# A two-layer transformer trunk: the Fourier stage's squares summed by TensorE, its additions by VectorE, none of them on GpSimd

## The chip, the cores and the metric

The kernel runs on one core of a Trainium2 chip. The metric is the device time of one execution in microseconds (us), given as the median of several runs. Five engines work at once, each through its own queue in order: TensorE (PE in the profile, its weight loads PEld), VectorE (DVE), ScalarE (ACT), GpSimd (POOL) and SyncE (SP), which issues most transfers.

## The reference

Two layers over 512 tokens of 1024 channels. Layer 0 is attention and a gated feed-forward network with a width-3 convolution; layer 1 is a Fourier mixer and another such network. Every sub-layer stands between two RMS norms. What this case touches is the end of layer 0 and the start of layer 1:

```
def rms_norm(x, g):
    y = xf * lax.rsqrt(jnp.mean(xf * xf, axis=-1, keepdims=True) + EPS)
    return (y * g.astype(F32)).astype(x.dtype)
...
def fourier_mix(h):
    hg = h.reshape(b, l, FNET_GROUPS, d // FNET_GROUPS).astype(F32)
    f = jnp.fft.fft2(hg, axes=(1, 3), norm="ortho").real
...
    x = x + g2 * rms_norm(conv_ffn(h, ...), norm_g[0, 3])        # end of layer 0
    h = modulate(rms_norm(x, norm_g[1, 0]), sh1, sc1)            # start of layer 1
    y = fourier_mix(h) @ w_f
```

All values are 32-bit floats.

## The kernel before

Activations lie transposed: 128 partitions hold 128 channels, the 1024 channels are 8 chunks (k = 0..7), and the 512 tokens run along the free axis in two halves of 256. The stream is `xT`, a sub-layer's output `yT`. For precise products each operand is split into a rounded part and a remainder (`hh`, `hl`; `wh`, `wl`; `zh`, `zl`), and `mm3` (L104 to L106) issues three matmuls into one PSUM tile. The PSUM pool has six tiles named `mm` and two named `misc`. A scheduler puts the written program into one order for each engine; `fence`, `held` and `follow` pin a few instructions.

**End of layer 0.** `ffn` ends with the down projection of its last group: eight output chunks `part(d)`, 8 x 3 matmuls of 128x256 each. All first halves (and d = 0 whole) come first. Then `mid(ys)` is called, and only after it in the written program stand the second halves of d = 1..7, 7 x 24 = 168 matmuls:

```
            if end:
                mid(ys)
                for d in range(1, KC):
                    part(d, [1])
```

Here `mid` is `plain.tiles(y, 0, 0, 3, pps, n1[0])`, the first token half's passage into layer 1. `ys.sums` has TensorE add up the squares of y (L187), `stat_bcast` turns them into a factor for each token (L205 to L209, L230, spread over partitions by the matmul L233, copied by ScalarE at L234), and for each chunk k:

- `x_update`: L317 scales y into `md_t` on VectorE, L319 adds it to `xT`, on VectorE for even k and on GpSimd for odd k in this first half;
- L372 (ScalarE) and L373 (VectorE) write the scaled new x, split into `hh` and `hl`;
- L380 (ScalarE) squares the new x, and L382 (GpSimd) adds the squares of chunks 1 to 6 into `yT[:, 0]`; chunks 0 and 7 are kept in `yT[:, 0]` and `yT[:, 7]`.

`columns` later sums these two tiles over the channels with four matmuls against a column of ones (L392), and `rstd` makes of them one factor for each token, with tokens on the partitions: the norm's factor is multiplied in only after the first Fourier product.

**Fourier stage.** `over_channels(g, h)` is the product over channels of group g and token half h (24 matmuls for the two token chunks of a half); `shift` computes the modulation's constant share (12 small matmuls, their inputs named `sh`); `group` and `cosines` are the products over tokens, for the first half's tokens (`[0, 1]`) and then for the second's (`[2, 3]`). The second half's `plain.tiles(ys, 1, ..., V)` runs between the first half's products, pumped piece by piece; there all of L319 is on VectorE already. The second half's Fourier products need no norm factor, but its tables do (`tables(1, r1)`, L1530 and L1531), so `columns(1)` stands ahead of them.

Last, `fourier_weights(d)` for d = 0..7 adds and subtracts two 128x512 blocks of the output weights (L1591 and L1592; L1591 by GpSimd but for d = 0), splits the result (L127, 128x1024), and 27 matmuls make output chunk d; L1651 and L1655 write it, and `ys.add` squares it on ScalarE (L290) and adds it up on GpSimd (L292, d = 1..5). GpSimd also issues the transfers of the next layer's first weights there (L1148, L1152, L1158).

Of the kernel before, what the change touches and what calls it, by code (L numbers as in the profile page):

```python
# [10 lines left out]
F32 = mybir.dt.float32  # L11
# [3 lines left out]
AF = mybir.ActivationFunctionType  # L15
ALU = mybir.AluOpType
# [3 lines left out]
P = 128  # L20
D = 1024
KC = D // P
T = 512
TT = T // P
HT = T // 2
# [56 lines left out]
def kernel(ctx: ExitStack, tc: tile.TileContext, a):  # L82
    nc = tc.nc
    V, S, G, PE, SY = nc.vector, nc.scalar, nc.gpsimd, nc.tensor, nc.sync
# [3 lines left out]
    def mk(pool, shape, dt=F32, tag=None, bufs=1):  # L88
        cnt[0] += 1
        n = nbufs.setdefault((id(pool), tag), (pool, bufs))[1]  # L90
        return pool.tile(shape, dt, tag=tag, name=f"{tag}_{cnt[0]}", bufs=n)
# [17 lines left out]
    def follow(i, j):  # L109
        tc.add_manual_dep(i.ins, j.ins.name, mybir.DependencyInfo(  # L110
            mybir.DependencyClass.NoSync, mybir.DependencyReason.DATA), reason="order")
# [19 lines left out]
    cp = ctx.enter_context(tc.tile_pool(name="cp", bufs=1))  # L131
# [14 lines left out]
    xT = mk(cp, [P, KC, T], F32, "xT")  # L146
    yT = mk(cp, [P, KC, T], F32, "yT")
# [3 lines left out]
    ones32 = mk(cp, [P, 32], F32, "ones32")  # L151
# [50 lines left out]
    def rstd(ps):  # L202
        w = ps.shape[1]
        v, t, r = (mk(cp, [P, W4], F32, "st_" + c, n)[:, :w] for c, n in (("v", 2), ("t", 1), ("r", 2)))
        S.activation(out=r, in_=ps, func=AF.Abs_reciprocal_sqrt, bias=eps, scale=1.0 / D)  # L205
        V.tensor_scalar(out=v, in0=ps, scalar1=1.0 / D, scalar2=EPS, op0=ALU.mult, op1=ALU.add)
        V.tensor_tensor(out=t, in0=r, in1=r, op=ALU.mult)
        V.scalar_tensor_tensor(out=t, in0=t, scalar=-0.5, in1=v, op0=ALU.mult, op1=ALU.mult)
        V.scalar_tensor_tensor(out=v, in0=t, scalar=1.5, in1=r, op0=ALU.add, op1=ALU.mult)  # L209
        return v  # L210
# [136 lines left out]
    class Plain:  # L347

        def __init__(self):
            self.acc = yT[:, 0, :]  # L350
            self.last = yT[:, KC - 1, :]

        def tiles(self, ys, h, l, gi, pps, am, urgent=False, eng=None, pe=False):
            hs = halves[h]
            ps = ys.sums(pps, h)
            if urgent:
                warm = mk(pps, [P, T], F32, "mm", 6)
                for s, n in zip(halves, HOT2):
                    busy(warm, ys.sq[:, s], n)
            R = stat_bcast(ps, pps)  # L360
            if urgent:
                busy(warm, R, HOT2[2])
            if pe and h == 0:
                self.ps = mk(pps, [P, T], F32, "mm", 6)
            yield
            for k in range(KC):
                i = x_update(h, l, gi, R, k, eng)
                if urgent and k == 1:
                    follow(i[0], j)
                j = i[1]  # L370
                x = xT[:, k, hs]
                S.activation(out=hh[:, k, hs], in_=x, func=AF.Copy, scale=am[:, k:k + 1])  # L372
                V.scalar_tensor_tensor(out=hl[:, k, hs], in0=x, scalar=am[:, k:k + 1], in1=f(hh[:, k, hs]),  # L373
                                       op0=ALU.mult, op1=ALU.subtract)
                if pe:
                    stat_x(self.ps[:, h * W4:], h, k)
                else:
                    sq = mk(cp, [P, T], F32, "sq", 2)[:, :HT] if 0 < k < KC - 1 else (self.last if k else self.acc)[
                        :, hs]
                    S.activation(out=sq, in_=x, func=AF.Square)  # L380
                    if 0 < k < KC - 1:
                        G.tensor_tensor(out=self.acc[:, hs], in0=self.acc[:, hs], in1=sq, op=ALU.add)  # L382
                if k % 2:
                    yield


        def columns(self, h, pps):
            ps = mk(pps, [P, T], F32, "misc", 2)
            for i in range(2):
                t = 2 * h + i  # L390
                for n, s in enumerate((self.acc, self.last)):
                    PE.matmul(ps[:, 2 * i:2 * i + 2], lhsT=s[:, t * P:(t + 1) * P], rhs=ones32[:, :2], start=n == 0,  # L392
                              stop=n == 1)
            return rstd(ps[:, :4])

        def rows(self, h):
            return rstd(self.ps[:, h * W4:(h + 1) * W4])
# [165 lines left out]
    def pump(it, n=1):  # L563
        for _ in range(n):
            next(it, None)
# [12 lines left out]
    with ExitStack() as es:  # L578
# [27 lines left out]
        with ExitStack() as e1:  # L606
            pj = e1.enter_context(tc.tile_pool(name="pj", bufs=1, reuse_waits="tile"))
            pps = e1.enter_context(tc.tile_pool(name="pps", bufs=1, space=PSUM, reuse_waits="tile"))
# [47 lines left out]
            for n in range(WARM):  # L656
                PE.matmul(warm[:, :256], lhsT=maskb[:, 0, :], rhs=maskb.rearrange("p a b -> p (a b)"), start=True,
                          stop=True)
# [100 lines left out]
            for s in START.split():  # L759
                n = [int(c) for c in s[1:]]  # L760
# [71 lines left out]
            for ps, (sh, sl, t, b) in zip(acc, tiles):  # L832
# [3 lines left out]
                if sh is ch:  # L836
                    sq = mk(cp, [P, T], F32, "sq", 2)[:, :256]
                    S.activation(out=sq, in_=src[:, 0, :], func=AF.Square)
                    V.tensor_tensor(out=dst.rearrange("p t (h d) -> p (t h) d", d=P),
                                    in0=src.rearrange("p t (h d) -> p (t h) d", d=P),  # L840
                                    in1=gqk[:, P:2 * P].unsqueeze(1).to_broadcast([P, 2, P]), op=ALU.mult)
# [48 lines left out]
            for g, kind in enumerate(["kb", "vb", "qa"]):  # L890
# [5 lines left out]
                for sh, sl, t0, kb in (blocks if kind[0] != "q" else blocks[:2]):  # L896
                    ps = mk(pps, [P, 2, 256], F32, "mm", 6)
# [26 lines left out]
        with ExitStack() as e2:  # L924
# [80 lines left out]
            for head in range(8):  # L1005
# [6 lines left out]
                for j in range(TT):  # L1012
                    qs = slice(j * P, (j + 1) * P)
                    ps = S0.pop() if S0 else mk(aps, [P, 1024], F32, "S", 2)
                    pr = mk(at, [P, NK], F32, "P", 7)
                    mx = mk(at, [P, 6], F32, "mx", 6)
                    if is_a:
# [4 lines left out]
                        reg, n = ps[:, 128:896], NK  # L1022
                    else:
# [9 lines left out]
                        for n_, (mi, off) in enumerate(mt):  # L1033
                            PE.matmul(ps[:, 512 + off:512 + off + P], lhsT=identb, rhs=maskb[:, mi, :],
                                      start=False, stop=n_ == len(mt) - 1)
                        reg, n = ps[:, 256:512 + nl], TC + nl
# [30 lines left out]
                    i = 4 * (head - 6) + j  # L1067
# [22 lines left out]
    pps = ctx.enter_context(tc.tile_pool(name="fps", bufs=1, space=PSUM, reuse_waits="tile"))  # L1090
    n0 = (der[:, 0, 2, :], mods[:, 0, 3, :])
    n1 = (der[:, 1, 0, :], mods[:, 1, 0, :])
# [377 lines left out]
    with ExitStack() as es:  # L1470
        xp = Pairs(es).rest(es)
        ys = out_proj(xp, ys, ow)
        plain = Plain()
        ys = ffn(0, xp, [], lambda: pump(boundary(ys, 1, 0, 1, pps, n0), 100),
                 lambda y: pump(plain.tiles(y, 0, 0, 3, pps, n1[0]), 6),
                 gemv_jobs([(1, v) for v in range(5)], pps, away))


    with ExitStack() as es:
# [103 lines left out]
            SY.dma_start(out=r, in_=a["w_f"][d])  # L1583
            return r

        def fourier_weights(d, eng=G):
            r = f_first[d] if d < 2 else raw([P, 4, 2, P], a["w_f"][d])

            pm = (yT[:, 6:8, :] if d in (3, 5) else yT[:, 2:4, :] if d == 1 else mk(cp, [P, 2, T], F32, "gacc")).rearrange(
                "p a (g c) -> p a g c", g=4)  # L1590
            held(eng.tensor_tensor(out=pm[:, 0, :, :], in0=r[:, :, 0, :], in1=r[:, :, 1, :], op=ALU.add))  # L1591
            held(V.tensor_tensor(out=pm[:, 1, :, :], in0=r[:, :, 1, :], in1=r[:, :, 0, :], op=ALU.subtract))  # L1592
            wh, wl = wpair([P, 2, 4, P])
            split(wh, wl, pm)
            return wh, wl
# [28 lines left out]
        group(2, [2, 3])  # L1624
        fence()
        group(0, [2, 3])
        w_f = [fourier_weights(0, V)]
        group(1, [2, 3])
        cosines(None, N, [z[:, :, :, P] for z in Z], list(range(TT)), fb[:4, 4:5])
        group(3, [2, 3])  # L1630
# [33 lines left out]
    with ExitStack() as es:  # L1664
# [13 lines left out]
        for k in range(0, KC, 2):  # L1678
            t = mk(cp, [P, T], F32, "sq", 2).rearrange("p (a b) -> p a b", a=2)
# [97 lines left out]
```

## Time and profile before

| | |
|---|---|
| median of 3 runs | 1136.24 us (1133.64 to 1137.02) |
| the profiled execution's own time | 1138.32 us |
| its span in the trace | 1136.5 us |
| TensorE matmul busy | 1098.6 us, 97% |
| VectorE busy | 902.6 us, 79% |
| ScalarE busy | 592.9 us, 52% |
| GpSimd busy | 174.9 us, 15% |
| mean granted TensorE clock | 0.991 |

A row of the engines' timeline reads: start in us from the span's start, duration in us, engine, line, operation, output<-inputs, shapes, count, and in brackets how long the engine had been idle before it and what released it. A matmul's end is modelled, so back-to-back matmuls overlap in these rows; their spacing is what they cost. A 32-bit matmul that isn't split appears as two passes. A row of the windows view reads: stretch, length, and busy time with the count of instructions of PE, PEld, DVE, ACT and POOL, then the granted clock, the DMA share and GB/s. A row of the groups reads: line, engine, operation, names, shapes, count, busy us, mean ns of one, and idle us before them.

### The profile page before, as it was taken

The page shows a single profiled execution, that of the slowest core. Times are in us where ns is not written, and L with a number is a line of the kernel's source. Part 1 is how long each engine was busy: PE and PEld are TensorE (multiplying, and loading weights), DVE is VectorE, ACT ScalarE, POOL GpSimd, SP SyncE. Part 2 cuts the span into 40 slices and gives each one's busy share as a digit, 9 for nine tenths or more (in the row PEclk, how much of TensorE's full clock was granted, in tenths as well). Part 3 has the DMA queues.
Part 4 walks back from the last instruction along what each step waited for, and adds up shares of the span by engine and source line. Part 5 has one row for each costly group of instructions (what it writes and reads, how often), then busy time and mean ns, then how long its engine had stood idle before and what let it go on. Part 6 is the DMA issues. An engine that isn't in the chain of part 4 may idle for free.

```text
span 1136.5 us, 19542 instructions
## 1 busy us (share of the span) xinstructions
PE 1098.6 (97%) x7810; PEld 962.9 (85%) x7810; DVE 902.6 (79%) x1469; ACT 592.9 (52%) x1056; POOL 174.9 (15%) x180
## 2 busy tenths in 40 slices
PE   9999899999999999999999999889999999999995
PEld 5689888868898978887998998779888898899995
DVE  5678777773789976978998568878997998879755
ACT  4342355665665633552555446557745555555543
POOL 1136422422320000000000153610000000000012
PEclk9999999999999999999999999899999999999998
DMA  9676101174142455536425302732114523222332
GB/s 365 262 238 216 38 1 39 53 274 156 63 162 111 156 204 203 181 131 236 187 75 204 103 20 75 206 114 108 74 47 160 192 103 116 103 89 95 105 144 75
DMA packets 33764, 155.83 MB, mean 137 GB/s; under 512 B 3461, under 2 KB 8197, under 8 KB 22025
## 3 DMA queue, kind: packets, MB, share of 16 engines
q1 hardware_dynamic: 32520, 150.39, 36.8%
q0 software_dynamic: 1152, 4.19, 1.6%
q8 instruction: 61, 1.00, 0.3%
q14 instruction: 31, 0.25, 0.1%
HBM read 148.28 MB, written 6.29 MB: 136 GB/s over the span
## 4 chain that ended last, share of the span: by engine, by line
PE 73%; DVE 15%; ACT 5%; DMA 3%; issue 2%; POOL 1%; SPq 0%; DVEq 0%; POOLq 0%; ACTq 0%
PE mm L104 21%; PE mm L106 20%; PE mm L105 20%; DVE wl L127 2%; DVE md_t L317 2%; PE PT L969 1%; ACT wh L127 1%; PE gm L104 1%; PE O L105 1%; DMA raw<-in_w_up 1%; PE gm L106 1%; PE gm L105 1%; ACT hh L251 1%; PE O L104 1%; DVE cv L1286 1%
## 5 line engine op out<-in xcount | busy, mean ns | idle before, releaser
L127 ACT CAST wh<-raw 128x1024 fp32r<-128x1024 f32 (+2 forms) x207 | 190.6, 933 | 168.8 <-PE mm L105 113.0
L127 DVE TENSOR_TENSOR wl<-raw,wh 128x1024 fp32r<-128x1024 f32 (+2 forms) x197 | 214.6, 1097 | 52.2 <-ACT wh L127 51.9
L104 PE MATMUL mm<-hh,wh 128*128 128x256 f32 (+1 forms) x632 | 204.5, 324 | 3.0 <-ACT sq L1224 1.5
L106 PE MATMUL mm<-hh,wl 128*128 128x256 f32 (+1 forms) x632 | 202.1, 320 | 0.4 <-DVE wl L127 0.2
L105 PE MATMUL mm<-hl,wh 128*128 128x256 f32 (+1 forms) x632 | 201.5, 319 | 0.0
L292 POOL TENSOR_TENSOR gacc<-gacc,sq 128x256 f32<-128x256 f32 (+1 forms) x33 | 28.0, 848 | 715.3 <-ACT sq L290 714.6
L104 PEld LDWEIGHTS mm<-hh,wh 128*128 128x128 f32 x632 | 118.6, 188 | 17.6 <-ACT sq L1224 5.6
L106 PEld LDWEIGHTS mm<-hh,wl 128*128 128x128 f32 x632 | 118.6, 188 | 10.6 <-DVE wl L127 1.0
L105 PEld LDWEIGHTS mm<-hl,wh 128*128 128x128 f32 x632 | 118.7, 188 | 9.9
L104 PE MATMUL mm<-zh,wh 128*128 128x256 f32 x384 | 109.5, 285 | 1.5 <-ACT sq L1227 0.9
L104 PE MATMUL mm<-xh,wh 128*128 128x512 f32 (+1 forms) x302 | 107.1, 355 | 0.0
L106 PE MATMUL mm<-zh,wl 128*128 128x256 f32 x384 | 107.1, 279 | 0.0
L105 PE MATMUL mm<-zl,wh 128*128 128x256 f32 x384 | 107.0, 279 | 0.0
L105 PE MATMUL mm<-xl,wh 128*128 128x512 f32 (+1 forms) x302 | 106.5, 353 | 0.0
L106 PE MATMUL mm<-xh,wl 128*128 128x512 f32 (+1 forms) x302 | 106.2, 352 | 0.0
L104 PEld LDWEIGHTS mm<-zh,wh 128*128 128x128 f32 x384 | 72.1, 188 | 5.8 <-ACT sq L1227 4.4
L106 PEld LDWEIGHTS mm<-zh,wl 128*128 128x128 f32 x384 | 72.5, 189 | 0.0
L105 PEld LDWEIGHTS mm<-zl,wh 128*128 128x128 f32 x384 | 72.1, 188 | 0.0
L104 PEld LDWEIGHTS mm<-xh,wh 128*128 128x128 f32 x302 | 56.7, 188 | 9.4 <-issue 1.6
L105 PEld LDWEIGHTS mm<-xl,wh 128*128 128x128 f32 x302 | 56.7, 188 | 8.5 <-issue 0.4
L106 PEld LDWEIGHTS mm<-xh,wl 128*128 128x128 f32 x302 | 56.8, 188 | 8.1
L1285 ACT ACTIVATE cv<-mm,cols 128x512 f32<-128x512 f32 x59 | 45.7, 777 | 23.8 <-PE mm L106 17.6
(435 smaller groups left out, 2793.8 us busy)
## 6 DMA issues: line engine op xcount, KB each, us to landing
raw<-in_w_up SPq DMA_DIRECT2D x42, 1024.0 KB, 4.9
xT<-in_mod_r SPq DMA_DIRECT2D x20, 1024.0 KB, 5.0
raw<-in_w_down SPq DMA_DIRECT2D x32, 384.0 KB, 3.0
raw<-in_mod_p SPq DMA_DIRECT2D x8, 1024.0 KB, 4.9
raw<-in_w_down SPq DMA_DIRECT2D x16, 512.0 KB, 3.9
raw<-in_w_in SPq DMA_DIRECT2D x6, 1024.0 KB, 8.1
yT<-in_mod_r SPq DMA_DIRECT2D x10, 512.0 KB, 6.4
raw<-in_w_out SPq DMA_DIRECT2D x4, 1024.0 KB, 5.4
```

Of the source, the lines that this page charges most:

```text
L104: i = PE.matmul(out, lhsT=ah, rhs=bh, start=start, stop=False, skip_group_check=skip)
L105: PE.matmul(out, lhsT=ah, rhs=bl, start=False, stop=False, skip_group_check=skip)
L106: return i, PE.matmul(out, lhsT=al, rhs=bh, start=False, stop=stop, skip_group_check=skip)
L127: i = S.copy(out=h, in_=src), eng.tensor_tensor(out=l, in0=src, in1=f(h), op=ALU.subtract)
L251: S.activation(out=h, in_=t, func=AF.Identity, bias=bm, scale=1.0)
L292: G.tensor_tensor(out=self.acc[:, sl], in0=self.acc[:, sl], in1=sq[:, sl], op=ALU.add)
L317: m = V.scalar_tensor_tensor(out=t, in0=yT[:, k, hs], scalar=der[:, l, gi, k:k + 1], in1=R, op0=ALU.mult, op1=ALU.mult)
L969: PE.transpose(out=pt[:, j * P:(j + 1) * P], in_=Ps[j][:, off:off + P], identity=ident)
L1285: S.activation(out=cv, in_=ps, func=AF.Identity, bias=bc, scale=wc[1])
L1286: V.scalar_tensor_tensor(out=cv[:, 1:], in0=ps[:, :T - 1], scalar=wc[0], in1=cv[:, 1:], op0=ALU.mult, op1=ALU.add)
```

## The change

Three kinds of work leave GpSimd around the Fourier stage:

- The squares of x. L380 squares two chunks in one ScalarE instruction of 128x512. For each such pair TensorE sums the squares with four matmuls against the column of ones (L384 of the changed kernel), all accumulated into one PSUM tile `col[h]`, taken from the six `mm` tiles when the first pair is reached. L382 goes, and so do the four matmuls of `columns`, whose `rstd` now reads `col[h]`.
- In the first token half the odd chunks' additions to x (L319) are VectorE's too.
- L1591 is VectorE's for every d.

Line numbers move: the old L372 and L373 are L371 and L372 in the changed kernel, and behind `columns` every number is higher by three (L1591 becomes L1594, L1592 L1595, L1651 L1654, L1655 L1658).

```
     def __init__(self):
-        self.acc = yT[:, 0, :]
-        self.last = yT[:, KC - 1, :]
+        self.col = {}
 ...
                 if pe:
                     stat_x(self.ps[:, h * W4:], h, k)
-                else:
-                    sq = mk(cp, [P, T], F32, "sq", 2)[:, :HT] if 0 < k < KC - 1 else (self.last if k else self.acc)[
-                        :, hs]
-                    S.activation(out=sq, in_=x, func=AF.Square)
-                    if 0 < k < KC - 1:
-                        G.tensor_tensor(out=self.acc[:, hs], in0=self.acc[:, hs], in1=sq, op=ALU.add)
+                elif k % 2:
+                    if k == 1:
+                        self.col[h] = mk(pps, [P, T], F32, "mm", 6)
+                    sq = mk(cp, [P, T], F32, "sq", 2)
+                    S.activation(out=sq.rearrange("p (a b) -> p a b", a=2), in_=xT[:, k - 1:k + 1, hs],
+                                 func=AF.Square)
+                    for c in range(2):
+                        for i in range(2):
+                            m = PE.matmul(self.col[h][:, 2 * i:2 * i + 2],
+                                          lhsT=sq[:, (2 * c + i) * P:(2 * c + i + 1) * P], rhs=ones32[:, :2],
+                                          start=k == 1 and c + i == 0, stop=k == KC - 1 and c == 1,
+                                          skip_group_check=True)
+                            if k == 1 and c == 0:
+                                if i:
+                                    follow(m, begun)
+                                begun = m
 ...
     def columns(self, h, pps):
-        ps = mk(pps, [P, T], F32, "misc", 2)
-        for i in range(2):
-            t = 2 * h + i
-            for n, s in enumerate((self.acc, self.last)):
-                PE.matmul(ps[:, 2 * i:2 * i + 2], lhsT=s[:, t * P:(t + 1) * P], rhs=ones32[:, :2], start=n == 0,
-                          stop=n == 1)
-        return rstd(ps[:, :4])
+        return rstd(self.col[h][:, :4])
 ...
-             lambda y: pump(plain.tiles(y, 0, 0, 3, pps, n1[0]), 6),
+             lambda y: pump(plain.tiles(y, 0, 0, 3, pps, n1[0], False, V), 6),
 ...
-    def fourier_weights(d, eng=G):
+    def fourier_weights(d, eng=V):
 ...
-    w_f = [fourier_weights(0, V)]
+    w_f = [fourier_weights(0)]
```

The scheduler's order of instructions moves at three places.

**TensorE at the end of layer 0.** In the kernel before, the second halves of the down projection (names `xh`, `xl` with `wh`, `wl`) stand between the sums of y's squares (L187), and 36 of their 168 matmuls lie between the first of these sums and the spreading matmul L233:

```order
L106 MATMUL mm_6925<-xh_6587,wl_6922 128x256
L187 MATMUL misc_6953<-gacc_6735,ones_8_71 32x64 x4
L104 MATMUL mm_7035<-xh_5921,wh_6683 128x256
L105 MATMUL mm_7035<-xl_5922,wh_6683 128x256
L106 MATMUL mm_7035<-xh_5921,wl_6684 128x256
...
L187 MATMUL misc_6953<-sq_6951,ones_8_71 32x64 x4
L105 MATMUL mm_7035<-xl_6124,wh_6683 128x256
...
L233 MATMUL misc_6972<-Rs_6970,con_66 128x256
L104 MATMUL mm_7064<-xh_6383,wh_6746 128x256
```

In the changed kernel the same place reads as follows, with `shift`'s 12 matmuls (`sh`) and the first sums of x's squares (L384) ahead of the first of the 168:

```order
L106 MATMUL mm_6925<-xh_6587,wl_6922 128x256
L187 MATMUL misc_6953<-gacc_6735,ones_8_71 32x64 x4
L187 MATMUL misc_6953<-sq_6951,ones_8_71 32x64 x4
L233 MATMUL misc_6972<-Rs_6970,con_66 128x256
L104 MATMUL misc_7286<-sh_1067_7282,wh_7258 128x4
...
L106 MATMUL misc_7286<-wh_7258,sh_1068_7283 4x2
L384 MATMUL mm_6985<-ones_8_71,sq_6986 128x2 x4
L104 MATMUL mm_7040<-xh_5921,wh_6683 128x256
```

So no matmul of the down projection stands between the sums of y's squares and the first sums of x's squares; the other three L384 groups stand among the 168.

**TensorE in the second half.** Before, the product over channels goes on around L233:

```order
L105 MATMUL mm_7390<-wl_7254,hh_69 128x256
L233 MATMUL misc_7339<-Rs_7337,con_66 128x256
L106 MATMUL mm_7390<-wh_7253,hl_70 128x256
L104 MATMUL mm_7390<-wh_7253,hh_69 128x256
L105 MATMUL mm_7390<-wl_7254,hh_69 128x256
```

Now L384 stands right behind L233, ahead of the remaining products over channels of the first token half:

```order
L106 MATMUL mm_7359<-wh_7258,hl_70 128x256
L233 MATMUL misc_7339<-Rs_7337,con_66 128x256
L384 MATMUL mm_7386<-ones_8_71,sq_7387 128x2 x4
L104 MATMUL mm_7393<-wh_7258,hh_69 128x256
L105 MATMUL mm_7393<-wl_7259,hh_69 128x256
```

Behind this L384 stand 60 large matmuls, the next L384, 24 more, and then the last two.

**VectorE in the weights' part.** Before, each d has L1592 alone on VectorE:

```order
L127 TENSOR_TENSOR wl_7840<-yT_68,wh_7839 128x1024
L1592 TENSOR_TENSOR gacc_7883<-raw_7881 128x512
L1592 TENSOR_TENSOR yT_68<-raw_7929 128x512
L1651 TENSOR_TENSOR yT_68<-mm_7811,qs_7827 128x256
L127 TENSOR_TENSOR wl_7887<-gacc_7883,wh_7886 128x1024
```

Now both operations of a d stand there, and the output of chunk d = 2 (`mm_7811`) stands between those of d = 4 (`raw_7881`) and d = 5:

```order
L127 TENSOR_TENSOR wl_7840<-yT_68,wh_7839 128x1024
L1658 TENSOR_TENSOR yT_68<-mm_7765,qs_7781 128x255
L1594 TENSOR_TENSOR gacc_7883<-raw_7881 128x512
L1595 TENSOR_TENSOR gacc_7883<-raw_7881 128x512
L1654 TENSOR_TENSOR yT_68<-mm_7811,qs_7827 128x256
L1594 TENSOR_TENSOR yT_68<-raw_7929 128x512
L1595 TENSOR_TENSOR yT_68<-raw_7929 128x512
L1658 TENSOR_TENSOR yT_68<-mm_7811,qs_7827 128x255
L127 TENSOR_TENSOR wl_7887<-gacc_7883,wh_7886 128x1024
```

SyncE's order is the same in both kernels.

## The prediction

> **What bounds the kernel now.** I read the chain of waits first: of the whole span 73% is TensorE's own time.
>
> ```profile
> PE 73%; DVE 15%; ACT 5%; DMA 3%; issue 2%; POOL 1%; SPq 0%; DVEq 0%; POOLq 0%; ACTq 0%
> ```
>
> So an edit counts by what it does to TensorE's queue, and VectorE's 15% tell where to look for the rest. Next come the windows over the changed part, cut at the stages' borders: the end of layer 0 (656 to 680), the second token half (685 to 703), the weights' part (from 710).
>
> ```profile
> 656.00:663.00 7.00, 5.81 (x57) 5.23 (x56) 3.11 (x7) 2.63 (x4) 1.27 (x1) 1.00 0.00 0
> 663.00:680.00 17.00, 17.00 (x154) 17.00 (x152) 15.20 (x27) 9.82 (x26) 11.99 (x14) 1.00 0.04 11
> 685.00:703.00 18.00, 16.38 (x129) 15.31 (x128) 15.92 (x38) 11.23 (x28) 5.78 (x6) 1.00 0.18 59
> 714.00:721.00 7.00, 7.00 (x30) 6.35 (x31) 3.65 (x6) 1.60 (x5) 2.77 (x2) 0.53 1.06 346
> 721.00:747.00 26.00, 24.01 (x194) 21.64 (x197) 20.32 (x23) 15.76 (x28) 16.32 (x13) 1.00 0.83 228
> ```
>
> From 663 to 680 TensorE never stops, although VectorE and GpSimd are at their fullest: the 168 matmuls of the second halves cover the first token half's passage. Whatever becomes faster there on VectorE is worth nothing, and whatever takes the cover away costs its full time. From 685 to 703 TensorE idles little (1.6 us), yet waits for VectorE's chain. In the last two rows something else shows: 30 matmuls took 7.00 us at a granted clock of 0.53, 0.233 us each, against 24.01 / 194 = 0.124 us at 1.00.
>
> **Term A: the end of layer 0.** TensorE's and the other engines' timelines there:
>
> ```profile
> 656.05 0.32 PE L187 MATMUL misc<-gacc,ones 128*32 128x64 f32 x8
> 656.30 0.39 PE L104 MATMUL mm<-xh,wh 128*128 128x256 f32 x1
> 657.32 0.32 PE L187 MATMUL misc<-sq,ones 128*32 128x64 f32 x8
> 660.93 0.28 PE L106 MATMUL mm<-xh,wl 128*128 128x256 f32 x1
> 662.40 0.67 PE L233 MATMUL misc<-Rs,con 128*128 128x256 f32 x2 [1.19 <-DVE Rs L230]
> 678.34 0.95 PE L392 MATMUL misc<-ones,yT 128*128 128x2 f32 x8
> 679.97 0.37 PE L104 MATMUL mm<-wh,hh 128*128 128x256 f32 x1
> ```
> ```profile
> 657.11 1.28 ACT L205 ACT_TABLE_LOAD   x1
> 658.40 0.31 ACT L205 ACTIVATE st_r<-misc,eps 128x64 f32<-128x64 f32 x1
> ```
> ```profile
> 658.89 0.22 DVE L207 TENSOR_TENSOR st_t<-st_r 128x64 f32<-128x64 f32 x1
> 659.85 0.42 DVE L1311 TENSOR_TENSOR yT<-yT,mm 128x256 f32<-128x256 f32 x1 [0.75 <-PE mm L106]
> 660.19 0.22 DVE L208 SCALAR_TENSOR_TENSOR st_t<-st_t,st_v 128x64 f32<-128x64 f32 x1
> 661.83 0.42 DVE L230 TENSOR_TENSOR Rs<-st_v,con 128x256 f32<-128x256 f32 x1
> ```
>
> Before, the matmuls ran from 656.30 to 678.34 with L187, a pause and L233 among them; 168 at the 0.1174 us of their spacing are 19.7 us. In the new order they stand behind L187, L233, `shift` and the first L384, and the queue runs in order. L187 ends at 657.4 and then TensorE has nothing but to wait for L233. The chain to it is short now, since VectorE's L1311, which waited for a matmul of the cover, no longer stands in it: L207 ends at 659.1, L208 and L209 at 0.22 each and L230 at 0.42 bring L233 to 660.1. From L233 to the first sums of x's squares the trace has a place of the same make in the next layer (factor copied, L317, L319, L372, square, sum):
>
> ```profile
> 750.10 0.67 PE L233 MATMUL misc<-Rs,con 128*128 128x256 f32 x2
> 754.79 0.65 PE L187 MATMUL mm<-sq,ones 128*32 128x64 f32 x16 [1.88 <-ACT sq L196]
> 757.05 0.42 PE L105 MATMUL mm<-hl,xh 128*128 128x258 f32 x1
> ```
>
> That is 4.7 us; with `shift` inside, L384 starts at 664.8. One L384 group is four 32-bit matmuls with a 128x128 load each, what the L392 row is: 0.95 us. So the cover starts at 665.7 in place of 656.3. Three more L384 groups lie among it (1.0 us each with the change of shapes): it ends at 665.7 + 19.7 + 3.0 = 688.4, 10.1 us later. Behind it the second half's L233, before at 684.56, is 2.8 us nearer: L392 and `shift` (1.6 us) no longer stand there, nor VectorE's steps for them. **A = +7.3 us.** Bounds: +5.5, if L233 to L384 takes 3 us, to +9.
>
> **Term B: the second token half.** Before, from L233 to the first product over the second half's tokens:
>
> ```profile
> 684.56 0.70 PE L233 MATMUL misc<-Rs,con 128*128 128x256 f32 x2 [0.49 <-DVE Rs L230]
> 702.86 0.86 PE L104 MATMUL mm<-ct,Z 128*128 128x258 f32 x4 [0.27 <-ACT ct L1530]
> ```
>
> 18.3 us, by VectorE's chain. Now TensorE's order decides: the first L384 at 4.7 us behind L233 with nothing between, then 60 large matmuls, an L384, 24, two L384s, 36: 4.7 + 4 x 0.95 + 120 x 0.118 = 22.7 us. VectorE, freed of GpSimd, would be through with x some 3 us sooner, but its result waits in TensorE's queue. **B = +4.4 us**; bounds 0 (the pause covered) to +6.
>
> **Term K: the clock.** The pause of 1.88 us before 754.79, in a stretch of small matmuls, was enough for 0.42 us where 0.28 is normal; a spacing of 0.21 against 0.12 over some nine matmuls cost 0.9 us. The stretch 714 to 721 cost 30 x (0.233 - 0.124) = 3.3 us. The new pauses (2.7 and 3.1 us in A with 1.6 us of small work between, 4.0 us in B) are larger. I take the middle, 1.9, for A, and 0.9 for B, where a slower TensorE partly fills waits: **K = +2.8 us**; bounds 0 to 6.6.
>
> The Trainium skill, "TensorE: Matmul & The Clock Gate", section on what is actually happening, has the clock halve only after an idle window of about 3.4 us. By that rule neither pause in A would do it, K would be about 0 and the sum 1146; the row at 754.79, where 1.88 us did, speaks against it.
>
> **Term C: the weights' part and GpSimd's collisions.** The groups from 663 to 745, and one operation alone and one beside GpSimd:
>
> ```profile
> L317 DVE SCALAR_TENSOR_TENSOR md_t<-yT,der,Rs 128x256 f32<-128x256 f32 x16 | 9.7, 628 | 1.6 <-ACT Rs L234 1.6
> L1592 DVE TENSOR_TENSOR gacc<-raw 128x512 f32<-128x512 f32 x4 | 6.9, 1722 | 0.0
> L127 DVE TENSOR_TENSOR wl<-yT,wh 128x1024 fp32r<-128x1024 f32 x3 | 5.3, 1754 | 0.0
> L382 POOL TENSOR_TENSOR yT<-yT,sq 128x256 f32<-128x256 f32 x12 | 10.7, 895 | 9.6 <-ACT sq L380 9.2
> L292 POOL TENSOR_TENSOR acc<-acc,sq 128x512 f32<-128x512 f32 x5 | 8.0, 1605 | 0.9 <-ACT sq L290 0.9
> L1591 POOL TENSOR_TENSOR gacc<-raw 128x512 f32<-128x512 f32 x4 | 6.5, 1617 | 9.8 <-DVE wl L127 9.8
> ```
> ```profile
> 714.94 0.68 DVE L1592 TENSOR_TENSOR yT<-raw 128x512 f32<-128x512 f32 x1
> 731.67 3.10 DVE L1592 TENSOR_TENSOR gacc<-raw 128x512 f32<-128x512 f32 x1
> ```
> ```profile
> 731.50 1.48 POOL L1591 TENSOR_TENSOR gacc<-raw 128x512 f32<-128x512 f32 x1
> 732.76 1.45 POOL L292 TENSOR_TENSOR acc<-acc,sq 128x512 f32<-128x512 f32 x1
> ```
>
> The 3.10 us operation lasted just until both GpSimd ones were over. Summed over these groups and the smaller ones of the same kinds, VectorE loses some 15 us to GpSimd from 663 to 745, about 9 of them in the weights' part. There the change takes seven L1591 from GpSimd and gives VectorE 7 x 0.60 = 4.2 us (0.60 is the spacing of the 0.68 us rows); L292 and the transfers' issue stay on GpSimd. For each d VectorE then has two L1591/L1592, one split (1.2) and two outputs (0.8), 3.2 us, against 3.6 of TensorE, the spacing of these two rows:
>
> ```profile
> 740.93 0.38 PE L104 MATMUL mm<-N,wh 4*128 4x258 f32 x1
> 744.53 0.38 PE L104 MATMUL mm<-N,wh 4*128 4x258 f32 x1
> ```
>
> So VectorE just keeps up, and what can be won is TensorE's waits for the splits:
>
> ```profile
> 724.16 0.39 PE L104 MATMUL mm<-B,wh 128*128 128x256 f32 x1 [0.50 <-ACT wh L127]
> 731.47 0.38 PE L106 MATMUL mm<-B,wl 128*128 128x256 f32 x1 [0.87 <-DVE wl L127]
> 735.96 0.38 PE L106 MATMUL mm<-B,wl 128*128 128x256 f32 x1 [0.62 <-DVE wl L127]
> ```
>
> 2.0 us. **C = -2.0 us.** Bounds: 8 x 3.6 = 28.8 us of matmuls fit in the 36.5 from 710.2 to 746.7, so at best -7.7 (both waits and slow clock gone); at worst +4.2, if VectorE, still beside L292, becomes the bound by all it was given. The four additions to x now on VectorE (0.34 us spacing, 1.4 in all) cost only the one in the chain to the first L384, counted there; the others lie under the 168 matmuls. ScalarE's squares, eight of 128x512 for sixteen of 128x256, take less of an engine with time to spare: 0. GpSimd's L382, 10.7 us, lay under TensorE's work in the first half (12 of 17 us busy, TensorE full) and goes for 0 there.
>
> **Sum.** 7.3 + 4.4 + 2.8 - 2.0 = +12.5 us on a span of 1136.5. The profiled execution took 1138.32, 1.8 more than its span and 2.1 above the median shown; the step goes on the median: 1136.24 + 12.5 = 1148.7, forecast **1148.5 us**.
>
> **Rivals.**
> - *The clock holds* (0.15): the pauses cost only themselves, +9.7, 1146. For it: pauses of 1.19 us (before L233) left the clock at 1.00 from 663 on. Against: 754.79. It is the case that the skill's rule above names.
> - *VectorE becomes the bound in the weights' part* (0.12): its 3.2 us for each d plus up to 1.3 of waiting for an L292 pass TensorE's 3.6; C turns to +4.2, sum +18.7, 1155. For it: 20.32 of 26 us busy already; against: most of that excess is L1591's.
> - *Faster: the collisions were the bound* (0.06): the 15 us that VectorE lost come back on the path, less 4.2 and 1.4 given to it, -9.4, 1127. It decides if TensorE's pause in A stays under some 1 us, that is if x's first pair is squared before the sums are needed; the order leaves nothing to run in that time, and TensorE was full while most collisions happened.
> - The remaining 0.05 is a half return of these, near 1136: B and K at zero, C at its best.
>
> The Trainium skill, "SBUF — State Buffer", lets VectorE and GpSimd exclude each other for a whole instruction when both read two SBUF inputs; the row of 3.10 us agrees. Taken alone it promises the third rival's 1127.
>
> **Numbers.** The forecast has 0.62; its own range is 1141 to 1155. With the slow rival nearly whole and the clock rival inside, 1140 to 1155.5. This measurement can't tell less than about 0.3% (3.4 us) from no change: slower 0.62 + 0.15 + 0.12 = 0.89, same 0.05, faster 0.06.
>
> **What would show it.** A: TensorE idle near 657.4 to 660.1 and 661.7 to 664.8 ahead of the first L384, the granted clock near 0.5 behind it, and the first `mm<-wh,hh` near 690. B: a pause of about 4 us behind the second L233, released by ScalarE's square, and 22 us from it to the first product over the second half's tokens. C: L1592 near 0.7 us and the splits near 1.2, without the 0.87 and 0.62 waits. I am wrong if the 168 matmuls cover the first token half after all, or if the 36.5 us of the weights' part shrink by over 7.

## The result: 14 us longer, and where they are

The changed kernel takes 1150.23 us in the median (1149.03 to 1152.97; a fifth execution, at a mean granted clock of 0.746, took 1358.12 us and is in neither this range nor the ratio) against 1135.77 of the kernel before; the ratio is 1.0128, with a 95% interval from 1.0112 to 1.0145. The forecast was 1148.5. The profiled execution's span grew from 1136.5 to 1148.5 us, and TensorE's share of the chain of waits from 73% to 77%:

```profile
PE 77%; DVE 12%; ACT 5%; DMA 3%; issue 2%; POOL 1%; SPq 0%; DVEq 0%; POOLq 0%; ACTq 0%
```

The windows of the changed kernel: the first two are the prediction's own, the last two lie where the second token half and the weights' part have moved to (the columns are the length, the busy time of TensorE, its weight loads, VectorE, ScalarE and GpSimd, then the granted clock, the DMA share and GB/s):

```profile
656.00:663.00 7.00, 3.46 (x35) 2.86 (x33) 1.65 (x6) 2.09 (x4) 0.61 (x1) 0.80 0.01 2
663.00:680.00 17.00, 14.11 (x96) 14.01 (x97) 10.67 (x28) 6.97 (x14) 1.28 (x1) 0.68 0.00 1
698.00:723.00 25.00, 21.35 (x157) 20.95 (x158) 16.50 (x43) 12.41 (x28) 0.00 (x0) 0.86 0.13 43
730.00:760.00 30.00, 29.96 (x216) 26.94 (x215) 23.70 (x40) 18.24 (x35) 12.68 (x13) 1.00 0.94 268
```

Where TensorE was full from 663 to 680, it now has 96 matmuls for 154, and a granted clock of 0.68. The weights' part, in the last row, went the other way: 29.96 of 30 us busy. The rows of TensorE's timeline at the borders:

```profile
657.51 0.32 PE L187 MATMUL misc<-gacc,ones 128*32 128x64 f32 x8
661.69 1.19 PE L233 MATMUL misc<-Rs,con 128*128 128x256 f32 x2 [2.77 <-DVE Rs L230]
667.00 1.87 PE L384 MATMUL mm<-ones,sq 128*128 128x2 f32 x8 [2.89 <-ACT sq L380]
673.93 0.95 PE L384 MATMUL mm<-ones,sq 128*128 128x2 f32 x8
698.08 0.70 PE L233 MATMUL misc<-Rs,con 128*128 128x256 f32 x2 [0.32 <-DVE Rs L230]
702.35 1.87 PE L384 MATMUL mm<-ones,sq 128*128 128x2 f32 x8 [3.57 <-ACT sq L380]
729.82 0.28 PE L104 MATMUL mm<-B,wh 128*128 128x256 f32 x1
759.87 0.28 PE L106 MATMUL mm<-A,wl 128*128 128x258 f32 x1
```

The last two are the first and the last product of the weights' part. In the kernel before they stand here:

```profile
710.22 0.28 PE L104 MATMUL mm<-B,wh 128*128 128x256 f32 x1
746.51 0.28 PE L106 MATMUL mm<-A,wl 128*128 128x258 f32 x1
```

So every profile can be cut at the same four rows (a cut is at a row's start): the first L187 of the sums at the end of layer 0, the second half's L233, the first and the last product of the weights' part. The first stretch holds term A, the second B, the third C. Before: 684.56 - 656.05 = 28.51, then 25.66, then 36.29 us. After: 40.57, 31.74 and 30.05. That is **A + K +12.06, B + K +6.08, C -6.24**, together +11.9 of the 12.0 us by which the spans differ. Counting from the first L187 on leaves out 1.46 us by which the changed kernel was late already there, ahead of everything that was changed; in the profiles of this study that point lies anywhere from 655.83 to 657.59, and 1.4 us come back behind the weights' part. The medians differ by 14.5 us and not by 12.0, because the profiled execution of the kernel before took 1138.32 us, 2.5 above its median; against two more profiles of that kernel (10 and 11 below) the changed kernel's span is 15.1 and 15.5 us longer.

The two L384 rows of 1.87 us are the same four sums as the 0.95 us row: half the clock. The pauses of 2.77, 2.89 and 3.57 us ahead are those that the prediction named. From the first of these sums at 667.00 to 697.8 TensorE has no other pause, so the PSUM tile that the sums now hold for a whole token half kept nothing waiting there.

### The profile page after: what moved, and what is told of

Read it like the earlier page. It is cut to its first block, busy times and chain, and to the rows that moved or that the text cites. A ratio compares the mean times of both kernels' runs of the same rounds, so it can differ in the third digit from the quotient of the medians.

```text
span 1148.5 us, 19603 instructions
## 1 busy us (share of the span) xinstructions
PE 1108.4 (97%) x7858; PEld 974.0 (85%) x7858; DVE 895.0 (78%) x1480; ACT 592.2 (52%) x1048; POOL 147.6 (13%) x157
## 4 chain that ended last, share of the span: by engine, by line
PE 77%; DVE 12%; ACT 5%; DMA 3%; issue 2%; POOL 1%; SPq 0%; DVEq 0%; POOLq 0%; ACTq 0%
PE mm L104 22%; PE mm L106 21%; PE mm L105 20%; DVE wl L127 2%; DVE md_t L317 1%; PE PT L972 1%; PE gm L104 1%; PE O L105 1%; PE gm L106 1%; DMA raw<-in_w_up 1%; PE gm L105 1%; DMA raw<-in_w_kva 1%; ACT hh L251 1%; PE O L104 1%; PE mm L384 1%
## 5 line engine op out<-in xcount | busy, mean ns | idle before, releaser
L1314 DVE TENSOR_TENSOR yT<-yT,mm 128x256 f32<-128x256 f32 (+1 forms) x54 | 29.0, 545 | 41.1 <-PE mm L106 41.0
```

Source lines behind the costliest of these rows:

```text
L1314: V.tensor_tensor(out=yT[:, d, sl], in0=yT[:, d, sl], in1=ps[:, sl], op=ALU.add)
```

## The experiments

Each kernel's profile is cut at the four rows. The table has the three stretches (us), the median time, and the ratio to the kernel before in the same comparison. The times of 10 and 11 are those of single executions.

| kernel | end of layer 0 | second half | weights' part | time | ratio (95%) |
|---|---|---|---|---|---|
| before | 28.51 | 25.66 | 36.29 | 1135.8 | 1 |
| after | 40.57 | 31.74 | 30.05 | 1150.2 | 1.0128 (1.0112 to 1.0145) |
| 1 weights' sums only | 28.44 | 25.67 | 30.00 | 1129.7 | 0.9939 (0.9917 to 0.9961) |
| 2 squares' sums only | 41.32 | 30.76 | 31.61 | 1149.2 | 1.0135 (1.0094 to 1.0175) |
| 3 squares' sums in the second half | 28.52 | 32.30 | 30.04 | 1136.4 | 1.0006 (0.9996 to 1.0017) |
| 4 squares' sums late | 35.55 | 27.22 | 30.02 | 1137.4 | 1.0018 (1.0007 to 1.0030) |
| 5 A's pauses filled | 36.40 | 31.75 | 30.02 | 1146.1 | 1.0094 (1.0079 to 1.0109) |
| 6 without the squares' sums | 28.34 | 25.68 | 30.01 | 1132.1 | 0.9968 (0.9956 to 0.9979) |
| 7 two weights' sums | 28.45 | 25.63 | 32.88 | 1134.4 | 0.9987 (0.9977 to 0.9997) |
| 8 squares' sums in the first half | 39.66 | 25.73 | 30.01 | 1142.8 | 1.0063 (1.0048 to 1.0078) |
| 9 all pauses filled | 36.40 | 29.11 | 30.02 | 1143.7 | 1.0072 (1.0054 to 1.0090) |
| 10 before, second profile | 28.52 | 25.66 | 33.34 | 1135.1 | |
| 11 before, third profile | 28.51 | 25.66 | 34.81 | 1134.7 | |
| 12 as 1, again | 28.62 | 25.62 | 29.97 | 1131.0 | 0.9959 (0.9946 to 0.9973) |

### 1: the weights' sums alone

On the kernel before:

```diff
-        def fourier_weights(d, eng=G):
+        def fourier_weights(d, eng=V):
```

> The kernel before with one part of the change: L1591 of the weights' part on VectorE for every d; squares, sums and additions as before. Theory (the 6.3 us that the weights' part lost between the two profiles come from this edit alone): about 1129.5 us against 1135.8, the part at 30 us in place of 36.5, no stretch at a clock near 0.5 behind 714, L1592 at 0.7 us but where L292 runs. Rival 1 (half of it was the clock, whose slow stretch went because the work ahead of it changed): the stretch 714 to 721 stays at 0.53, about 1132.5. Rival 2 (VectorE, given seven additions, becomes the bound when nothing ahead is delayed): 1136 or more.

It took 1129.7 us, as the theory has it, and is faster than the kernel before. A and B are untouched (28.44 and 25.67), the weights' part is at 30.00. Two windows of it; the second answers to the row of 0.53 in the prediction:

```profile
710.00:740.00 30.00, 29.61 (x217) 26.72 (x216) 25.60 (x42) 19.24 (x36) 13.49 (x13) 1.00 0.96 272
714.00:721.00 7.00, 7.00 (x55) 6.46 (x54) 6.78 (x12) 4.75 (x10) 0.90 (x1) 1.00 1.00 359
```

TensorE is busy for 29.61 of 30 us, VectorE for 25.60. With all eight sums VectorE is not the bound.

### 2: the squares' sums alone

On the changed kernel:

```diff
-                 lambda y: pump(plain.tiles(y, 0, 0, 3, pps, n1[0], False, V), 6),
+                 lambda y: pump(plain.tiles(y, 0, 0, 3, pps, n1[0]), 6),
...
-        def fourier_weights(d, eng=V):
+        def fourier_weights(d, eng=G):
...
-        w_f = [fourier_weights(0)]
+        w_f = [fourier_weights(0, V)]
```

> The changed kernel with two of its three parts undone: the weights' sums and the first half's additions to x on GpSimd again; only the squares' sums on TensorE. Theory (A and B are the price of L384's places in TensorE's queue, and C is another part's gain): no gain of 6.3 is there to set against them, 1135.8 + 18 = 1154 us, the 36 us of the weights' part as before. Rival (the additions on VectorE and the weights' sums delay VectorE's chain and make A and B larger): 1146 or less.

A and B are there in full, 12.8 and 5.1 us, so the rival falls. But the time is 1149.2, not 1154 (which the interval, 1146 to 1155, still holds): the weights' part takes 31.61 us, though GpSimd makes its sums. Its only wait of note is at the start:

```profile
730.83 0.38 PE L105 MATMUL mm<-B,wh 128*128 128x256 f32 x1 [2.16 <-DVE B L127]
```

TensorE comes 18 us late, and most of GpSimd's delay has presumably passed before it arrives. That C is owed to moving L1591 holds only where A and B cost nothing; within the whole change the move is worth 31.61 - 30.05 = 1.6 us. Why the later waits of 0.87 and 0.62 us are gone here too is not settled.

### 3 and 8: one token half each

On the changed kernel, with the lines of the kernel before put back for the other half (8 has `h != 0`):

```diff
+                elif h != 1:
+                    sq = mk(cp, [P, T], F32, "sq", 2)[:, :HT] if 0 < k < KC - 1 else (self.last if k else self.acc)[
+                        :, hs]
+                    S.activation(out=sq, in_=x, func=AF.Square)
+                    if 0 < k < KC - 1:
+                        G.tensor_tensor(out=self.acc[:, hs], in0=self.acc[:, hs], in1=sq, op=ALU.add)
                 elif k % 2:
...
         def columns(self, h, pps):
+            if h != 1:
...
+                return rstd(ps[:, :4])
             return rstd(self.col[h][:, :4])
```

> The changed kernel with the first token half's sums of squares done as before the change (ScalarE squares, GpSimd adds, four matmuls at the end); the second half, the additions and the weights' sums stay changed. Theory (A is 12 us and belongs to the first half's sums alone): the 168 matmuls cover the first half again, and B and C are left, 1135.8 + 6.3 - 6.3 = 1136 us. Rival (A comes from the additions on VectorE, or the second half takes over the pause): 1145 or more.

> The changed kernel with the second token half's sums of squares done as before the change; the first half, the additions and the weights' sums stay changed. Theory (A 12 us, B 6, C -6 simply add up): 1135.5 + 12 - 6 = 1141.5 us. Rival (the halves depend on each other: what the first half delays, the second finds ready, or the other way): 1139 or less, or 1144 or more.

Both came out by the theory, the second 1.3 us above its 1141.5: 1136.4 and 1142.8 us. With the first half's sums as before, the cover is back; the windows of that kernel:

```profile
663.00:680.00 17.00, 17.00 (x153) 17.00 (x153) 15.42 (x33) 10.05 (x26) 9.18 (x10) 1.00 0.08 21
685.00:710.00 25.00, 21.43 (x157) 21.27 (x157) 15.89 (x41) 12.15 (x27) 0.00 (x0) 0.86 0.14 43
```

A belongs to the first half's sums and B to the second's, and each leaves the other stretch as it was (28.52 and 25.73).

### 4: the sums late

On the changed kernel the squares are kept, in columns of yT that are free by then, and all sixteen sums of a half are issued where the four stood before the change:

```diff
+    LATE = (0, 1)
...
+                elif k % 2 and h in LATE:
+                    S.activation(out=self.kept(h, k), in_=xT[:, k - 1:k + 1, hs], func=AF.Square)
                 elif k % 2:
...
         def columns(self, h, pps):
+            if h in LATE:
+                ps = mk(pps, [P, T], F32, "misc", 2)
+                for i in range(2):
+                    for k in range(KC):
+                        PE.matmul(ps[:, 2 * i:2 * i + 2], lhsT=self.kept(h, k | 1)[:, k % 2, i * P:(i + 1) * P],
+                                  rhs=ones32[:, :2], start=k == 0, stop=k == KC - 1)
+                return rstd(ps[:, :4])
```

> The changed kernel with the same number of sum matmuls, but all 16 of a half issued in one row where the four matmuls on the running sums stood before the change; the squares of all channels are kept until then in the columns of yT that the additions to x have already read. Theory (A and B are the order: a queue that stands at the first sum while the covering products wait behind it): both go, 24 more matmuls at 0.24 us stay, 5.7 us, and C's 6.3 us are won: 1135.8 + 5.7 - 6.3 = 1135 us, TensorE busy from 663 to 680. Rival (A and B are the price of the sums themselves, of small matmuls with a fresh load, wherever they stand): 1146 or more.

1137.4 us: 2.4 over the theory, 9 under the rival. Of the 18.1 us of A, B and the clock, 5.0 + 4.5 go with the order alone; 7.0 and 1.6 stay, where the theory had 5.7 for both. TensorE's rows and windows there show why:

```profile
679.47 4.88 PE L412 MATMUL misc<-ones,yT 128*128 128x2 f32 x32
684.21 0.35 PE L104 MATMUL misc<-sh,wh 128*128 128x4 f32 x1
691.16 0.41 PE L105 MATMUL mm<-wl,hh 128*128 128x256 f32 x1
691.38 0.41 PE L106 MATMUL mm<-wh,hl 128*128 128x256 f32 x1
```
```profile
663.00:679.00 16.00, 15.47 (x131) 15.45 (x131) 12.46 (x31) 9.03 (x19) 3.18 (x4) 1.00 0.10 32
679.47:681.59 2.12, 2.12 (x22) 2.12 (x20) 0.42 (x1) 0.00 (x0) 0.00 (x0) 1.00 0.00 0
681.59:684.21 2.62, 2.62 (x14) 2.62 (x14) 0.00 (x0) 0.00 (x0) 0.00 (x0) 0.50 0.00 0
685.00:693.00 8.00, 8.00 (x72) 7.55 (x73) 3.70 (x14) 2.33 (x6) 1.19 (x1) 0.57 0.01 2
```

The sums take 684.21 - 679.47 = 4.74 us up to the next instruction. In the kernel before, the four sums of 678.34 take 0.80:

```profile
679.14 0.25 PE L104 MATMUL misc<-sh,wh 128*128 128x4 f32 x1
```

TensorE does not pause, and yet the clock falls, in the middle of the sums: their last 2.62 us run at half of it, and the products behind stand 0.21 us apart until 691.6. At the full clock the sums would take about 2.12 + 2.62 / 2 = 3.4 us. So of the 7.0 us that are left of A about 2.6 are the sums' own and 4.4 the clock's, an estimate from these rows; the theory had half of 5.7 for the sums and nothing for the clock.

### 5 and 9: useless work in the pauses

On the changed kernel (5 has the first two places, 9 all three; the sums of these matmuls are read by nobody):

```diff
+    DUMMY = [5, 5, 5]
...
+            filled = eng is V and not pe and h == 0
+            if filled:
+                warm = mk(pps, [P, T], F32, "mm", 6)
+            if filled:
+                busy(warm, ys.sq[:, halves[0]], DUMMY[0])
             R = stat_bcast(ps, pps)
+            if filled:
+                busy(warm, R, DUMMY[1])
...
                     if k == 1:
+                        if h:
+                            busy(mk(pps, [P, T], F32, "mm", 6), R, DUMMY[2])
                         self.col[h] = mk(pps, [P, T], F32, "mm", 6)
```

> The changed kernel with work of no use put into the two pauses of A: five 32-bit matmuls of 256 columns between L187 and L233, five between shift and the first L384, into a PSUM tile that nobody reads. Theory (of A's 12 us about 3.5 are the clock, which falls in the pauses and stays low for the first 24 covering matmuls): the granted clock stays at 1.00 from 656 to 680, 1150.2 - 3.5 = 1146.7 us, the pauses gone from the rows but the first L384 hardly earlier. Rival (the pauses cost only their length): 1149.5 to 1151 us.

> The kernel with the two pauses of A filled, and in addition five such matmuls of no use between the second half's L233 and its first L384. Theory (B's first sum and 18 products behind it ran at half the clock, 0.84 + 18 x 0.097 = 2.6 us): B 6.1 - 2.6 = 3.5 us, 1146.1 - 2.6 = 1143.5 us, no granted clock under 1.00 from 695 to 720. Rival (the low clock fell into time that VectorE's chain takes anyway): 1146 us again.

1146.1 and 1143.7 us, both as the theory has it. With A's pauses filled:

```profile
658.82 2.32 PE L181 MATMUL mm<-sq,ones 128*32 128x256 f32 x10
661.77 0.67 PE L233 MATMUL misc<-Rs,con 128*128 128x256 f32 x2 [0.63 <-DVE Rs L230]
663.09 2.35 PE L181 MATMUL mm<-Rs,ones 128*32 128x256 f32 x10
666.05 1.05 PE L393 MATMUL mm<-ones,sq 128*128 128x2 f32 x8 [0.61 <-ACT sq L389]
```
```profile
663.00:680.00 17.00, 16.39 (x135) 14.88 (x132) 13.29 (x34) 8.60 (x18) 2.95 (x3) 1.00 0.10 32
```

Counted from the first L187, the first sum (L393 here) starts 1.0 us earlier, since the small matmuls ahead of it are not stretched, and everything behind it runs at the full clock: 135 matmuls between 663 and 680, ten of them of no use, where the changed kernel has 96. The first stretch shrinks by 40.57 - 36.40 = **4.2 us**, the second, in kernel 9, by 31.75 - 29.11 = **2.6 us**. These are the two parts of K in the changed kernel's profile, measured by taking them away. The window of kernel 9 over the second half has the clock at 1.00:

```profile
695.00:720.00 25.00, 24.10 (x197) 22.77 (x198) 18.43 (x49) 13.14 (x30) 0.00 (x0) 1.00 0.24 85
```

K is not the same in every execution. Kernel 8 has the changed kernel's first half, and its stretch is 39.66 us, 3.3 above the filled one; in the second half kernels 2 and 3 are 1.7 and 3.2 above it. The clock fell in all three profiles with A's pauses open (after, 2, 8) and in all four with B's open (after, 2, 3, 5), and in none where they are filled (A in 5 and 9, B in 9).

### 6: the change without the squares' sums

On the kernel before, the edit of kernel 1 and

```diff
-                 lambda y: pump(plain.tiles(y, 0, 0, 3, pps, n1[0]), 6),
+                 lambda y: pump(plain.tiles(y, 0, 0, 3, pps, n1[0], False, V), 6),
```

> The change without its first part: weights' sums and the first half's additions to x on VectorE, the squares summed by GpSimd as before. Theory (the additions lie under the 168 covering matmuls, and A and B are the sums' alone): 1129.7 us, as with the weights' sums alone, within 1 us. Rival (the additions lengthen VectorE's chain of the first half, 4 x 0.34 us, and end the cover too early): 1131 us or more, with a wait behind the cover.

1132.1 us: the time is past the theory's bound of 1130.7 and in the rival's range, but the rival's sign is missing. The three stretches are 28.34, 25.68 and 30.01, each within 0.1 of kernel 1, and no wait stands behind the cover. The profiles' spans differ by 1.3 us, and 1.26 of it lie ahead of the first L187, where the two kernels do the same; kernel 12, the same code as 1, gave 1131.0. In the stretches no cost of the additions can be seen, and the intervals of 6 and 12 overlap.

### 7, 10, 11 and 12: the size of C

On the kernel before, only d = 0 and 1 on VectorE:

```diff
             r = f_first[d] if d < 2 else raw([P, 4, 2, P], a["w_f"][d])
+            eng = V if d < 2 else eng
```

> The kernel before with L1591 on VectorE for d = 0 and 1 only, the six others on GpSimd. Theory (of C's 6 us some 4.3 come from the start: the second split, late by GpSimd's first sum, whose waits of 0.36 and 0.62 us let the clock fall for 714 to 721; and 2.0 from later waits): 1135.5 - 4.3 = 1131.2 us, no stretch at 0.53, the waits of 0.5 to 0.9 us further on still there. Rival (each of the seven sums gives its share of the collisions): one seventh of 5.8, 1134.7 us, and the stretch at 0.53 stays.

The time was 1134.4, the rival's, but the stretch at 0.53 is gone: the part took 32.88 us at full clock. So neither had it. The waits of this kernel:

```profile
712.35 0.39 PE L106 MATMUL mm<-B,wl 128*128 128x256 f32 x1 [0.70 <-DVE wl L127]
713.75 0.38 PE L105 MATMUL mm<-N,wh 4*128 4x258 f32 x1 [0.22 <-DVE N L127]
721.81 0.38 PE L104 MATMUL mm<-B,wh 128*128 128x256 f32 x1 [0.39 <-ACT wh L127]
729.12 0.39 PE L106 MATMUL mm<-B,wl 128*128 128x256 f32 x1 [0.87 <-DVE wl L127]
733.60 0.38 PE L106 MATMUL mm<-B,wl 128*128 128x256 f32 x1 [0.62 <-DVE wl L127]
```

A wait of 0.70 us near the start remains, and still no fall of the clock. That made the row of 0.53 doubtful, so the kernel before was profiled twice more, unchanged:

> The kernel before, unchanged, for another profile of the weights' part. Theory A (the stretch at half the clock from 714 to 721 belongs to the order of this kernel): it is there again, the part takes 36.3 us. Theory B (the clock's fall there is a matter of the single execution, since the same waits in the kernel with two weights' sums moved did not bring it): the part takes 33.0 us and TensorE's waits for the splits alone make C, 3 us.

> The same once more, for a third profile of the kernel before: 36.3 us by theory A, 33.0 us or either by theory B.

Its two waits at the start and the window over the part, in the second profile and then in the third:

```profile
712.45 0.39 PE L106 MATMUL mm<-B,wl 128*128 128x256 f32 x1 [0.36 <-DVE wl L127]
714.68 0.38 PE L106 MATMUL mm<-B,wl 128*128 128x256 f32 x1 [0.61 <-DVE wl L127]
...
711.00:745.00 34.00, 31.23 (x223) 27.62 (x222) 28.27 (x35) 19.57 (x36) 23.57 (x20) 1.00 0.84 245
```
```profile
711.41 0.39 PE L106 MATMUL mm<-B,wl 128*128 128x256 f32 x1 [0.36 <-DVE wl L127]
713.63 0.38 PE L106 MATMUL mm<-B,wl 128*128 128x256 f32 x1 [0.61 <-DVE wl L127]
...
710.00:745.00 35.00, 32.26 (x219) 28.58 (x219) 28.29 (x35) 19.57 (x36) 23.53 (x20) 0.95 0.80 232
```

The same waits, 0.36 and 0.61 us, and three answers of the clock: no fall (33.34 us), a short one (34.81), a long one (36.29). Theory B holds. What the weights' sums win every time is 33.34 - 30.00 = 3.3 us: TensorE's waits in the part go from 2.8 us (profile 10) to 0.4 (kernel 1), and the rest is not separated. Kernel 7 wins 0.5 of it, though its five waits come to 2.8 us too. Up to 3 us more depend on the execution. In the time:

> The kernel with only the weights' sums moved to VectorE once more, with more rounds, for the size of C in the time. Theory A (only TensorE's waits for the splits go every time; the clock's fall at 714 is in some executions of the kernel before): 3.0 to 3.5 us, 0.997 of the kernel before. Theory B (the fall is in most executions and goes with them): 5 to 6 us, 0.995.

0.9959 of 1134.6 us is -4.7 us (-6.1 to -3.1), between the two theories' sizes, and the interval reaches both. That the fall is in some executions and not in others is shown by the three profiles, not by this time.

## Why the prediction was right, point by point

**A, the pauses and the cover: right.** The forecast was +7.3 without the clock. With the clock held up (kernel 5) the stretch is 36.40 us, +7.9. L187 to L233 has a pause of 2.77 us (forecast 2.7), L233 to the first sum takes 666.05 - 661.77 = 4.3 us at full clock (4.7). Kernel 3 shows that it belongs to the first half's sums, kernel 4 that 5.0 of the 12.06 us go when only their place in the queue changes; of the rest about 2.6 are their own time.

**B, the second half: right.** Forecast +4.4, with the clock held +3.45 (kernel 9); the pause ahead of the first sum was 3.57 us (about 4).

**K, the clock: the mechanism right, the size wrong.** The step that failed is "I take the middle, 1.9, for A, and 0.9 for B": K measured 4.2 + 2.6 = 6.8 us, just over the step's upper bound of 6.6 (and the middle of its two gauges, 0.9 and 3.3, is 2.1, not 1.9). Its gauge was nine matmuls at a spacing of 0.21; in A the first sum and 24 products ran slow, in B the first sum and 18. And "a slower TensorE partly fills waits" did not happen in B: 0.84 + 18 x 0.097 = 2.6 us of slow matmuls came back whole in kernel 9.

**C, the weights' part: the direction right, the size wrong.** The step that failed is the sum of three waits, "2.0 us". It left out the waits at the start, 0.36 and 0.62 us (2.97 in all), and put the clock's stretch into the bound alone. Measured: -3.3 us without the clock's fall, -6.2 in the two profiles compared, where the kernel before had the longest fall of three.

K is 4.0 us larger than forecast and C, in these profiles, 4.2 us more of a gain, so here the two errors cancel. That is luck, and it holds for these two profiles: with the second profile of the kernel before, which has no fall, C is -3.3 and the sum +14.8, and the medians moved by +14.5, 2.0 us above the forecast. C is not a term by itself either: late as the part comes in the changed kernel, it takes 31.61 us even with GpSimd's sums, so moving L1591 is worth 1.6 us there (kernel 2). A + B without the clock, 11.7 forecast and 11.3 measured, is the part that was understood.

**Costed at nothing:** x's additions and ScalarE's longer squares. For the additions kernel 6 bears it out while the cover lies over them, with 28.34 us against 28.44. No run separates ScalarE's longer squares.

**The rivals.** "The clock holds" gave 1146; kernel 9, where work was put in to hold it, took 1143.7, with the larger C. The changed kernel by itself does not hold it. The row quoted against this rival, half the clock behind a pause of 1.88 us, was no good evidence: in kernel 1 the same place has the same pause and the full clock:

```profile
748.23 0.43 PE L187 MATMUL mm<-sq,ones 128*32 128x64 f32 x16 [1.89 <-ACT sq L196]
```

The Trainium skill, "TensorE: Matmul & The Clock Gate", section on what is actually happening, has the clock judged in a free-running window of about 3.4 us. The answer to one pause would then depend on where the pause falls, and the three profiles of the kernel before agree. So does kernel 8: behind the same pause of 2.77 us its L233 still ran at the full clock, and the fall came 0.7 us later:

```profile
660.93 0.67 PE L233 MATMUL misc<-Rs,con 128*128 128x256 f32 x2 [2.77 <-DVE Rs L230]
...
661.63:671.87 10.24, 7.35 (x40) 7.25 (x40) 7.31 (x21) 3.73 (x8) 0.00 (x0) 0.50 0.00 0
```

In the changed kernel the clock was down before L233, and these are the last 3.41 us ahead of the fall and the whole of it:

```profile
656.75:660.16 3.41, 1.40 (x24) 0.95 (x22) 0.42 (x1) 1.99 (x3) 0.00 (x0) 1.00 0.00 0
660.16:673.81 13.65, 9.23 (x46) 8.98 (x47) 8.53 (x26) 3.75 (x9) 0.00 (x0) 0.50 0.00 0
```

The same section of the Trainium skill has the clock halve after an idle window of about 3.4 us; that it has to be idle does not hold here. In the changed kernel TensorE was busy for 1.40 of the 3.41 us ahead of the fall, no pause there was longer than 2.77, and in kernel 4 the clock fell with no pause.

"VectorE becomes the bound" falls with kernel 1 (25.60 of 30 us busy). "The collisions were the bound" was right for one of three edits: the weights' sums alone make the kernel faster than both.

## What to carry to other kernels

Before work goes to an engine that sits on the chain, look at what stands behind it in that engine's queue: sixteen small sums in place of four cost some 2.6 us by themselves, and 12 with the covering products that waited behind the first of them and the clock that fell meanwhile. A pause in TensorE costs its length and then the products that run slow behind it, here up to 4 us; filling the pause with matmuls of no use shows that second part and wins it back. Where edits are bundled, time each one alone: here the one that helps (the weights' sums, 0.9959) was hidden under the one that cost.

## What was not expected of the hardware

During sixteen sums of two columns in a row, 4.74 us without a pause, the granted clock fell to half, and it was 0.57 over the products behind them (kernel 4). Being busy by the profile is not enough to hold it; ten 256-column passes in 2.3 us in each of two pauses were (kernels 5 and 9). The same program with the same waits had the clock at half for seven microseconds, for part of that, or not at all (profiles before, 11 and 10). From the end of layer 0 to the end of the weights' part, every stretch at half clock in the fourteen profiles lasts 3.41, 6.83, 10.24 or 13.65 us, one to four times the same length: the clock changes in steps of time, and one more step costs a stretch full of products up to 1.7 us, an estimate (half of 3.41). So a stretch of low clock in one profile is no property of the kernel until a second profile has it.
